# A two-layer sequence trunk on one core: the copy of U on ScalarE alone, betas and keys scaled in place in two buffers

## The chip, the cores and the metric

The kernel runs on one core of one Trainium2 chip. The core has a matrix engine (PE in the profile, with its weight loads as PEld), a vector engine (DVE), a scalar engine (ACT), a general engine (POOL) and a queue that issues most transfers (SP). Each engine works through a list of its own in order and waits on semaphores where it needs another engine's result. The metric is the device time of one execution in microseconds (us). The kernel before took 1878.74 us (median of three runs, 1875.97 to 1879.16).

## The reference

The kernel computes two layers on 1024 positions of 1024 channels, in float32. Layer 0 has two recurrent mixers side by side; layer 1, which the change touches, is a delta rule with 16 heads of 64 channels. After the projections that make r, k, v, the decay w, the rate and the gate, the reference runs one step per position and head:

```python
def step(state, inp):
    r_t, w_t, k_t, v_t, al_t, be_t = inp
    sa = jnp.einsum("bhvk,bhk->bhv", state, al_t)
    state = (state * w_t[:, :, None, :] + sa[..., None] * be_t[:, :, None, :]
             + v_t[..., None] * k_t[:, :, None, :])
    return state, jnp.einsum("bhvk,bhk->bhv", state, r_t)
```

Here `al` is minus the normalised key, called alpha below, and `be` is that key times the rate, called beta. The outputs y then get a group norm, a bonus and a gate, the output projection, a row norm and the residual.

## The kernel before, in words

Layer 1 handles 16 chunks of 64 positions. Inside a chunk the recurrence is solved with matrices. `prep` (line 1144) writes, for each chunk, alphas and receptances to a DRAM tensor `ard` and betas and keys to `bkd`. `invert` (line 1264) inverts a triangular matrix of a chunk by row steps on DVE (lines 1294, 1297, 1303 and 1306), and `merge` (line 1313) finishes it on PE. The inversions are generators that are advanced between the steps of the chunks (`background`, line 1118), and all of them are done before chunk 8.

`chain_phase` (line 1023) runs the chunks one after another. For chunk ch it calls three functions:

- `values(ch + 1)` (line 1386) loads the values and the inverse of the next chunk.
- `gram(ch + 1)` (line 1399) loads `GM` (alphas and receptances) and `BK` (betas and keys) of the next chunk, multiplies them on PE (line 1415, 32 products in two groups of 16), and masks the products on DVE (lines 1420 and 1421). Then POOL multiplies all of `BK` with the decay at the chunk's end, `egc`, and writes the result to another tile, `BS` (line 1425). PE transposes `BS` in eight pieces (line 1430), and ACT copies them to `NK` (line 1431). `BK` and `BS` have one slot each in the pool `cb`, 4 KB per partition.
- `chain(ch)` (line 1434) carries the state. The tile `SV` holds the state of a head on its half of the partitions and values on the other half. PE multiplies it with the masked products (line 1443), ACT copies the result (line 1445), and PE multiplies it with the inverse (line 1458). The result is U, in one bank of PSUM. It replaces the state in `SV`: line 1460 copies the half of the even heads (partitions 0 to 63) with DVE and that of the odd heads with ACT. PE then forms the next state from U, the values and `NK` (line 1465), DVE adds the decayed old state `se` (line 1467), which POOL made (line 1454), and PE completes the outputs (line 1470), which ACT copies (line 1473).

Between these steps run pieces of other work: the gates (line 1013) up to chunk 8, then the group norms (`norm`, line 1479; its small steps are in `rstd2`, lines 201 to 206) and the output projection (`project`, line 1523).

Nobody writes the order of an engine's list by hand. The program opens with `tile.TileContext(nc, schedule_with_timeline_sim=True)` (line 1605): a planner simulates the kernel with durations of its own while it builds it. It puts every instruction into its engine's list when, in that simulation, its inputs and its slot are there, the earlier in the program the sooner. Line 1087 raises the priority of the last two chunks. On the chip each list then runs in that fixed order. A tile of a pool waits for its slot: with one slot, the next chunk's `BK` can be loaded only when the last reader of this chunk's `BK` is done.

Of the kernel before, what the change touches and what calls it, by code (L numbers as in the profile page):

```python
# [7 lines left out]
F32 = mybir.dt.float32  # L8
# [17 lines left out]
# columns of the packed per-channel vectors, eight columns each  # L26
# [6 lines left out]
class Steps:  # L33
    """a generator with the parts that it makes"""
# [11 lines left out]
class Net:  # L46
# [39 lines left out]
    # ---------------------------------------------------------------- constants  # L86
# [15 lines left out]
    def mask_from(self, pool, tmp, name, shape, conds):  # L102
        """uint8 mask, 1 where every affine condition (pattern, base, cm) >= 0 holds."""
        nc = self.nc
        n = 1
        for s in shape:
            n *= s
        m = tmp.tile([P, n], F32, name="mask_f")
        nc.gpsimd.memset(m, 1.0)
        view = m  # L110
        if len(shape) == 2:
            view = m.rearrange("p (a b) -> p a b", b=shape[1])
        for pat, base, cm in conds:
            nc.gpsimd.affine_select(out=view, in_=view, pattern=pat, compare_op=ALU.is_ge, fill=0.0,
                                    base=base, channel_multiplier=cm)
        u = pool.tile([P, n], U8, name=name)
        nc.vector.tensor_copy(u, m)
        return u

    # ---------------------------------------------------------------- weights  # L120
    def weights(self, units):
        """the pool of weights, for these units in this order; a unit is two pieces"""
        self.wp = self.ctx.enter_context(self.pool("wp", 4))
        self.order, self.queue = list(units), []
# [14 lines left out]
    def unit(self):  # L139
        """the next unit of weights in the order of use, its successor on the way"""  # L140
# [11 lines left out]
    def dense_t2(self, w, e, uh, ul, th):  # L152
        """[128 channels, 512 positions] of unit w's e-th column tile, in two steps."""
# [21 lines left out]
    def dense_n(self, w, uh, ul, tt):  # L175
        """[128 positions, 256 channels] of unit w."""
# [12 lines left out]
    def rstd(self, pool, ss, n, scale, eps):  # L189
        """(ss * scale + eps) ** -0.5 on [128, n]."""  # L190
# [6 lines left out]
    def rstd2(self, pool, ss, n, scale, eps):  # L197
        """the same by the square root of the scalar engine and a Newton step"""
# [10 lines left out]
    def norm_rows(self, pool, x, sq):  # L209
        """root-mean-square scale [128,1] of a row tile [128, 1024]."""  # L210
# [5 lines left out]
    # ---------------------------------------------------------------- layer 0  # L216
    def layer0(self):
        tc, nc, a = self.tc, self.nc, self.a
        with ExitStack() as cx:
            uh, ul = ([[self.mx.tile([P, HALF], F32R, name=f"x{n}{th}") for _ in range(KT)] for th in range(2)] for n in "hl")  # L220
            rgk = cx.enter_context(self.pool("rgk", 1))
            with ExitStack() as c2:
# [38 lines left out]
                # the first projections of the next part lie in PSUM until its pools are there  # L261
# [17 lines left out]
    def warm(self, pool, n):  # L279
        """products of zeros that keep the tensor engine's clock up until there is work"""  # L280
# [9 lines left out]
    def hgrn_consts(self, c, hp):  # L290
        nc = self.nc
        # lower bound and its complement, per channel
# [16 lines left out]
        # masks of a 64-block's rows and columns, the same in both halves of the partitions  # L309
# [6 lines left out]
        # (block, group of blocks, source block of a group)  # L316
# [9 lines left out]
    def hgrn_dense(self, c, big, uh, ul, trees):  # L326
        """the projections, in pieces; a tree starts when its queries and keys are there"""
# [61 lines left out]
    def advance(self, gens):  # L389
        """a stage of the first tree, at times one of the second too"""  # L390
# [5 lines left out]
    def hgrn_half(self, hp, stp, th, j, tr, st, diag, lev):  # L396
        """two heads, four blocks of 128 positions each; the heads run in step"""
        nc = self.nc
        # scores, transposed
# [3 lines left out]
        def scores(i, rhs, w, n, b):  # L403
            """products of the sources of a block of 64 with its groups of n blocks of b targets, w blocks apart"""
# [9 lines left out]
        def put(i, ps, w, b, g, s, mask, dst, src):  # L414
            """the blocks dst of every group of g from the slots src of every w, where the mask allows it"""
# [9 lines left out]
        def wider(i, b, pool):  # L425
            """sources with their way through the other half of a block of 2 * b, totals of such blocks"""
# [8 lines left out]
        # positions themselves and next ones  # L435
# [17 lines left out]
        # blocks of 4 * b from such of b: the slots of a group are queries of its blocks 0 to 3 (even ones) and those of  # L453
        # blocks 2, 3, 3 with their ways through block 1, blocks 1 and 2, block 2 (odd ones)
# [57 lines left out]
        for Q, F, K, V, G, row in tr:  # L512
            # keys with positions on partitions
# [54 lines left out]
    def gate_consts(self, c, tmp):  # L568
        """parts of the gates' matrices, a block of 64 channels at a time, both gates of it beside each other: high
        ones against the two parts of the block on the two halves of the partitions, low ones on the block's own half"""  # L570
# [15 lines left out]
    def rglru(self, cx, uh, ul):  # L586
        tc, nc, a = self.tc, self.nc, self.a
        # -8 softplus(-lam) per channel: max(-lam, 0) + log1p(exp(-|lam|))
# [19 lines left out]
        # sigmoids by tanh: sigmoid(z) = (1 + tanh(z / 2)) / 2  # L608
# [11 lines left out]
        for j in range(4):  # L620
# [45 lines left out]
            # the halves of the two sigmoids that are factors, squared  # L666
# [10 lines left out]
    def out0(self, cx):  # L677
# [9 lines left out]
        for th in range(2):  # L687
# [18 lines left out]
            for dh in range(2):  # L706
                ps = [self.pss.tile([P, HALF], F32, name="sm") if dh else self.psd.tile([P, HALF], F32, name="mm") for _ in range(4)]
                for gi, kg in enumerate(order):
                    w = self.unit()
                    # the last unit row tile by row tile, so that the first ones are there early  # L710
# [46 lines left out]
    def finish(self, rp, th, Y, ss):  # L757
        """norms and residual of four row tiles, and their channels on partitions"""
# [29 lines left out]
    def receptance(self, w, j, th, e2):  # L788
        """a column tile of r, in two steps"""
# [6 lines left out]
    # ---------------------------------------------------------------- layer 1  # L796
    def mix(self, p, k, th, out):
        """u + (shifted u - u) * mu for one channel tile and half."""
# [6 lines left out]
    def mix_parts(self, mp, p, th, eng=None):  # L805
        """the same, a channel tile at a step"""
# [13 lines left out]
    def mixes(self, mp, p, th, eng=None):  # L820
        """the parts of one half of a mix, in the slots of that half"""
# [8 lines left out]
    def lora_consts(self):  # L830
        """the first factors of decay and rate, times 1 - mu and times mu"""
# [16 lines left out]
    def lora(self, th):  # L848
        """low-rank decay and rate of one half"""
# [18 lines left out]
    def lora_parts(self, th, x):  # L868
        """the low parts of the decays on the second half of the partitions, those of the rates on the first"""
# [7 lines left out]
    def layer1_consts(self):  # L877
# [6 lines left out]
        # halves for sigmoids by tanh: 1 + (sigmoid - 1) k_a = tanh * k_a / 2 + 1 - k_a / 2  # L884
# [7 lines left out]
    def layer1_proj(self):  # L892
# [12 lines left out]
        with ExitStack() as cx:  # L905
            mp = self.mx
            with ExitStack() as c2:
                lp = c2.enter_context(self.pool("lora", 1))
                # parts of the low-rank factors: high ones twice, against the two parts of the other factor
# [32 lines left out]
                with ExitStack() as c3:  # L942
                    kp = c3.enter_context(self.pool("kp", 2))
                    # selectors that put a head's sum over its channels into its row: norms and bonuses, in them halves, in them heads
# [13 lines left out]
                    # three stages, one slot apart  # L958
# [29 lines left out]
    def pieces(self, piece, hi, lo):  # L988
        """the pieces of a projection, the first halves of two units before their second halves"""
# [10 lines left out]
    def vpiece(self, w, hi, lo, j, tt):  # L1000
        """values of a row tile, and their products with the bonus"""
# [11 lines left out]
    def gpiece(self, w, hi, lo, j, tt):  # L1013
        """gates of a row tile"""
# [8 lines left out]
    def chain_phase(self, cx, mp, vg, n):  # L1023
        """values with the first inversions; then the chunks one after another, among them the gates, the other
        inversions and, from the middle on, the output"""
# [107 lines left out]
    def output_weight(self, dh, i):  # L1133
        """(k, half of the columns) parts of the last weight, in the slots of the mixes"""
# [9 lines left out]
    def prep(self, kp, e, th, pk):  # L1144
# [13 lines left out]
        # sigmoid(z) = (1 + tanh(z / 2)) / 2  # L1158
# [5 lines left out]
        # running decay exponent inside each chunk, twice  # L1164
# [19 lines left out]
        # squared norms of the heads' keys  # L1184
# [11 lines left out]
        # beta . alpha inside the chunks, rows are source positions  # L1196
# [22 lines left out]
    def head_sums(self, kp, e, th, i, x):  # L1219
        """sums over the channels of the two heads, added to the rows of norms (i = 0) or bonuses"""  # L1220
# [9 lines left out]
    def norms(self, kp):  # L1230
        """bonuses with positions on partitions; inverse squared norms, halved, with 32-blocks on partitions"""
# [16 lines left out]
    def invert_consts(self):  # L1248
# [4 lines left out]
        # halved inverse squared norms, 32 positions to a row, in the order of the blocks  # L1253
# [3 lines left out]
        # identity rows of the 16-blocks, eight rows to a partition group  # L1257
# [6 lines left out]
    def invert(self, cp):  # L1264
        """(I - A)^-1, transposed, of two chunks: 32-blocks row by row on the vector engine, the last level on the
        tensor engine."""
# [5 lines left out]
        # columns times their inverse norms, and so those of the inverse  # L1272
# [14 lines left out]
        def solve(yo, nk, ao):  # L1287
            """columns 1..15 of nk blocks of YP from yo on, by the block of BL at ao"""
# [24 lines left out]
    def merge(self, ch):  # L1313
        """the last level of an inversion, on the tensor engine"""
# [38 lines left out]
    # ---------------------------------------------------------------- chunks  # L1353
    def chain_consts(self):
        nc, big = self.nc, self.big
        # causal masks: rows are source positions (twice), columns strict for alpha and inclusive for r
# [29 lines left out]
    def values(self, ch):  # L1386
        """state (or, later, U) on the head's half of the partitions, values on the other"""
# [11 lines left out]
    def gram(self, ch):  # L1399
# [5 lines left out]
        BK = self.big.tile([P, KT, P], F32, name="BK")  # L1405
# [17 lines left out]
        BS = self.big.tile([P, KT, P], F32, name="BS")  # L1423
        eg_ = self.egc[:, ch, :].rearrange("p (e o) -> p e o", o=1).broadcast_to([P, KT, P])
        nc.gpsimd.tensor_mul(BS, BK, eg_)
        NK = self.cc[ch % 2].tile([P, KT, P], F32, name="NK")
        for eg in range(2):
            ps = self.bank("pt").rearrange("p (q t) -> p q t", t=P)
            for q in range(4):
                nc.tensor.transpose(ps[:, q, :], BS[:, eg * 4 + q, :], self.ident)  # L1430
# [3 lines left out]
    def chain(self, ch):  # L1434
# [24 lines left out]
        for h in range(2):  # L1459
            (nc.scalar.copy if h else nc.vector.tensor_copy)(SV[H[h], h], ps[H[h]])  # L1460
# [18 lines left out]
    def norm(self, ch):  # L1479
        """group norm, bonus and gate of a chunk"""  # L1480
# [30 lines left out]
    def turn(self, ch):  # L1511
        """the two parts of a chunk's rows with channels on partitions"""
# [10 lines left out]
    def project(self, tt):  # L1523
        """output projection, norm and residual of a row tile; the next tile is made ready between"""
# [37 lines left out]
def pack(inputs):  # L1562
# [5 lines left out]
    # the value and gate channels in the order (head parity, head pair, channel), and so the rows of the output weight  # L1568
# [41 lines left out]
```

## Time and profile before

| what | value |
|---|---|
| runs | 1878.74 us median, 1875.97 to 1879.16 |
| span of the profiled execution | 1879.1 us, from the first to the last instruction |
| time of the profiled execution | not listed apart; the slowest run shown is 1879.16 us |
| mean granted PE clock | 0.940 |
| DVE, all copies of line 1460 | 16 of 0.675 us, 1398.2 to 1843.2 us |
| ACT, all copies of line 1460 | 16 of 0.580 us, 1399.0 to 1843.9 us |
| POOL, the scalings of line 1425 | 16 of 1.93 us, 1246.7 to 1815.9 us |
| loads of `BK` | 16 of 512 KB, 4.2 us to landing |

The time axis of the profile starts at the first instruction. Layer 0 and the projections take the first 1244 us; the values' projection with the first inversions goes on to about 1362 us, and the chunks run from there to the end. A row of the timeline gives the start, the duration, the engine, the line, the operation, and in brackets the idle time of the engine before it and what ended it. A row of the waits gives the waiting engine and line, what it waited for, the total in us, the number of waits and the longest one.

### The profile page before, as it was taken

The numbers are of one execution on the slowest core, as the hardware profiler recorded it, in microseconds if no ns is written. First come the engines' busy times: TensorE is split into PE (matmuls) and PEld (weight loads), VectorE is DVE, ScalarE is ACT, GpSimd is POOL, SyncE is SP. The second block draws the span as 40 slices with busy tenths as digits, with TensorE's granted clock in tenths as the row PEclk, the third lists the DMA queues.
The fourth block names the chain that finished last, engine by engine and source line by source line (L and its number), as shares of the span: only waits on it lengthen the run. The fifth ranks groups of instructions, "written<-read, shape, count | busy, mean of one in ns | idle before, by whom it ended". The sixth has DMA issues, their size and how long they took to land. (4 is left out here: it accounts for less than half of the span.)

```text
span 1879.1 us, 34525 instructions
## 1 busy us (share of the span) xinstructions
PE 1726.0 (92%) x13394; PEld 1447.4 (77%) x13394; DVE 1353.5 (72%) x2621; ACT 767.7 (41%) x1468; POOL 717.3 (38%) x638
## 2 busy tenths in 40 slices
PE   7989989999899999999999999979788879978888
PEld 6879789787897777777878766669787868867666
DVE  6585483675847889745355686885999999489984
ACT  5322222323226755545454765666452223242221
POOL 5534232333222212465434243555532333373530
PEclk9989999999899999999999999969889889788989
DMA  5101101111022111375332266756344444664531
GB/s 182 46 24 46 56 18 63 46 35 39 19 72 86 50 63 67 124 236 173 101 123 96 90 152 155 176 138 188 101 144 130 141 129 136 181 197 146 163 102 62
DMA packets 177491, 201.79 MB, mean 107 GB/s; under 512 B 91440, under 2 KB 122416, under 8 KB 177328
## 3 DMA queue, kind: packets, MB, share of 16 engines
q1 hardware_dynamic: 176176, 195.39, 34.9%
q0 software_dynamic: 1152, 4.19, 0.7%
q8 instruction: 106, 1.74, 0.4%
q14 instruction: 57, 0.47, 0.1%
HBM read 136.28 MB, written 63.24 MB: 106 GB/s over the span
## 5 line engine op out<-in xcount | busy, mean ns | idle before, releaser
L135 POOL TENSOR_TENSOR wl<-w,wh 128x1024 fp32r<-128x1024 f32 x110 | 275.5, 2511 | 288.7 <-ACT wh L133 280.6
L160 PE MATMUL mm<-xh,wh 128*128 128x512 f32 x768 | 306.8, 400 | 1.4 <-ACT KK L1183 1.4
L162 PE MATMUL mm<-xh,wl 128*128 128x512 f32 x768 | 305.4, 398 | 0.0
L161 PE MATMUL mm<-xl,wh 128*128 128x512 f32 x768 | 304.6, 397 | 0.0
L184 PE MATMUL mm<-wh,xh 128*128 128x256 f32 x560 | 170.6, 305 | 6.0 <-ACT xh L149 4.4
L160 PEld LDWEIGHTS mm<-xh,wh 128*128 128x128 f32 x768 | 145.6, 190 | 37.0 <-issue 3.9
L162 PEld LDWEIGHTS mm<-xh,wl 128*128 128x128 f32 x768 | 146.0, 190 | 35.3 <-issue 5.0
L186 PE MATMUL mm<-wh,xl 128*128 128x256 f32 x560 | 167.5, 302 | 5.0 <-DVE xl L150 4.3
L161 PEld LDWEIGHTS mm<-xl,wh 128*128 128x128 f32 x768 | 145.9, 190 | 33.3 <-issue 3.4
L185 PE MATMUL mm<-wl,xh 128*128 128x256 f32 x560 | 166.3, 297 | 0.0
L133 ACT CAST wh<-w 128x1024 fp32r<-128x1024 f32 x112 | 117.3, 1049 | 115.8 <-PE mm L161 57.1
L1294 DVE TENSOR_TENSOR PR<-YP,BL 128x80 f32<-128x80 f32 (+20 forms) x240 | 125.8, 545 | 14.1 <-POOL BL L1276 12.0
L184 PEld LDWEIGHTS mm<-wh,xh 128*128 128x128 f32 x560 | 115.0, 205 | 9.7 <-ACT xh L149 5.0
L186 PEld LDWEIGHTS mm<-wh,xl 128*128 128x128 f32 x560 | 114.5, 206 | 7.2 <-DVE xl L150 5.4
L185 PEld LDWEIGHTS mm<-wl,xh 128*128 128x128 f32 x560 | 114.9, 205 | 0.7
L184 PE MATMUL po<-wh,xh 128*128 128x256 f32 x256 | 80.8, 316 | 1.3 <-DVE vg L1020 1.3
L1415 PE MATMUL pg<-GM,BK 64*128 64x128 f32 x512 | 64.3, 328 | 17.0 <-DVE RB L1421 11.5
L185 PE MATMUL po<-wl,xh 128*128 128x256 f32 x256 | 79.5, 311 | 0.0
L186 PE MATMUL po<-wh,xl 128*128 128x256 f32 x256 | 78.2, 306 | 0.0
L803 DVE SCALAR_TENSOR_TENSOR mix<-ut,vec,mix 128x512 f32<-128x512 f32 x64 | 57.2, 902 | 27.6 <-ACT mix L802 26.8
L420 DVE COPY_PREDICATED ST<-m_l,sm 64x128 f32<-64x128 uint8 x224 | 72.4, 337 | 5.5
L1415 PEld LDWEIGHTS pg<-GM,BK 64*128 64x128 f32 x512 | 52.5, 222 | 23.0 <-issue 19.0
(374 smaller groups left out, 4355.7 us busy)
## 6 DMA issues: line engine op xcount, KB each, us to landing
w<-in_W SPq DMA_DIRECT2D x112, 512.0 KB, 3.7
ard<-AR SPq DMA_DIRECT2D x16, 512.0 KB, 4.1
BK<-bkd SPq DMA_DIRECT2D x16, 512.0 KB, 4.2
vd<-vg SPq DMA_DIRECT2D x32, 256.0 KB, 2.9
GM<-ard SPq DMA_DIRECT2D x32, 256.0 KB, 4.4
x<-in_x SPq DMA_DIRECT2D x8, 512.0 KB, 10.1
mgd<-sgq SPq DMA_DIRECT2D x16, 256.0 KB, 2.3
ut<-mgd SPq DMA_DIRECT2D x16, 256.0 KB, 4.5
```

Source lines behind the costliest of these rows:

```text
L133: nc.scalar.copy(hi, w)
L135: (nc.vector if first else nc.gpsimd).tensor_sub(lo, w, hi.bitcast(F32))
L160: nc.tensor.matmul(ps, lhsT=wh[:, c:c + P], rhs=a, start=(k == 0), stop=False)
L161: nc.tensor.matmul(ps, lhsT=wh[:, c:c + P], rhs=b, start=False, stop=False)
L162: nc.tensor.matmul(ps, lhsT=wl[:, c:c + P], rhs=a, start=False, stop=(k == KT - 1))
L184: nc.tensor.matmul(ps, lhsT=a, rhs=h, start=(k == 0), stop=False)
L185: nc.tensor.matmul(ps, lhsT=a, rhs=l, start=False, stop=False)
L186: nc.tensor.matmul(ps, lhsT=b, rhs=h, start=False, stop=(k == KT - 1))
L420: nc.vector.copy_predicated(d, m, x)
L803: nc.vector.scalar_tensor_tensor(out, sh, self.v(f"mu{p}", k), out, ALU.mult, ALU.add)
L1294: nc.vector.tensor_mul(pr, fv(YP, yo, kd + [[48, 8], [1, n]]), fv(BL, ao + i, k0 + [[0, 8], [32, n]]))
L1415: nc.tensor.matmul(ps[h][:, q, :], lhsT=BK[hs, eg * 4 + q, :], rhs=GM[hs, h, eg * 4 + q, :], start=True, stop=True)
```

## The change

Three lines of arithmetic change, all in the chunk loop. The copy of U goes through ACT for both halves. POOL writes the scaled betas and keys back into `BK`, and PE transposes `BK`; the tile `BS` is gone. `BK` gets two slots instead of one, so `BK` and `BS` together take as much memory as the two slots do. Comments and docstrings are left out too, which changes no instruction.

```diff
-        BK = self.big.tile([P, KT, P], F32, name="BK")
+        BK = self.big.tile([P, KT, P], F32, name="BK", bufs=2)
         nc.sync.dma_start(out=BK, in_=self.bkd[ch])
...
-        BS = self.big.tile([P, KT, P], F32, name="BS")
         eg_ = self.egc[:, ch, :].rearrange("p (e o) -> p e o", o=1).broadcast_to([P, KT, P])
-        nc.gpsimd.tensor_mul(BS, BK, eg_)
+        nc.gpsimd.tensor_mul(BK, BK, eg_)
         NK = self.cc[ch % 2].tile([P, KT, P], F32, name="NK")
         for eg in range(2):
             ps = self.bank("pt").rearrange("p (q t) -> p q t", t=P)
             for q in range(4):
-                nc.tensor.transpose(ps[:, q, :], BS[:, eg * 4 + q, :], self.ident)
+                nc.tensor.transpose(ps[:, q, :], BK[:, eg * 4 + q, :], self.ident)
             nc.scalar.copy(NK[:, eg * 4:eg * 4 + 4, :], ps)
...
         for h in range(2):
-            (nc.scalar.copy if h else nc.vector.tensor_copy)(SV[H[h], h], ps[H[h]])
+            nc.scalar.copy(SV[H[h], h], ps[H[h]])
```

## The prediction

> **What bounds the kernel now.** I began with the busy times and slices, to see which engine is full where the change acts.
>
> ```profile
> span 1879.1 us, 34525 instructions
> PE 1726.0 (92%) x13394; PEld 1447.4 (77%) x13394; DVE 1353.5 (72%) x2621; ACT 767.7 (41%) x1468; POOL 717.3 (38%) x638
> ...
> DVE  6585483675847889745355686885999999489984
> ```
>
> Each slice is 47 us; the chunk loop takes the last eleven. DVE stands at 9 in most of them, though its share of the whole span is only 72%. So I cut the loop into stretches; columns are length, busy time (instructions) of PE, weight loads, DVE, ACT, POOL, then clock and DMA.
>
> ```profile
> 1362.00:1597.00 235.00, 204.82 (x2926) 185.39 (x2925) 228.94 (x525) 72.08 (x152) 84.51 (x66) 0.88 0.48 136
> 1597.00:1644.00 47.00, 43.28 (x546) 38.87 (x546) 22.96 (x42) 11.91 (x25) 15.65 (x14) 0.78 0.66 182
> 1644.00:1832.00 188.00, 157.40 (x1661) 126.33 (x1661) 167.16 (x283) 50.81 (x112) 90.51 (x67) 0.88 0.50 152
> 1832.00:1879.00 47.00, 38.80 (x221) 28.85 (x221) 23.45 (x55) 9.23 (x25) 4.48 (x3) 0.96 0.18 62
> ```
>
> To 1597 us (chunks 0 to 7, with the inversions between) DVE works 228.94 of 235 us, 97%: it sets the pace. Chunks 9 to 14 have 167.16 of 188, 89%, with PE at 84%. Between (chunk 8) and in the tail DVE is half idle. Next the copy of U, by its line:
>
> ```profile
> L1460 DVE COPY SV<-pc x16: 670/675/683, 1398.2 to 1843.2; 64x512 f32<-64x512 f32 x16
> L1460 ACT COPY SV<-pc x16: 580/580/584, 1399.0 to 1843.9; 64x512 f32<-64x512 f32 x16
> ...
>   DVE SV L1460: 62.8, 13
>   issue: 5.6, 1
>   DVE rv L201: 3.4, 1
>   PE pc L1458: 2.2, 3
> ```
>
> Half of U goes through DVE (0.675 us), half through ACT (0.580 us), and ACT's half begins only after DVE's. ACT stood ready at this copy for 62.8 us in 13 of 16 chunks, waiting for a DVE copy that itself stood in DVE's queue (it waited for its product only 3 times, 2.2 us). Last, who waits behind it on PE, over the loop and then from 1644 us on:
>
> ```profile
> PE pc L1465 <- DVE SV L1460: 20.0, 6, 4.7
> PE pg L1415 <- DVE RB L1421: 11.5, 7, 4.0
> PE pg L1415 <- DMA BK<-bkd: 5.4, 1, 5.4
> ```
> ```profile
> PE pc L1465 <- DVE SV L1460: 11.7, 3, 4.4
> ```
>
> **The change, part by part.**
>
> *U by ScalarE alone.* DVE loses 16 × 0.675 = 10.8 us. What that is worth depends on the stretch. Chunks 0 to 6 copy before 1597 us: 7 × 0.675 × 0.97 = 4.6 us. Chunks 9 to 14: 6 × 0.675 × 0.89 = 3.6 us. Chunks 7, 8 and 15 fall where DVE has gaps; nothing is counted. Together **−8.2 us**. ACT gains 16 × 0.580 = 9.3 us of work. I cost that at nothing: in the two DVE-bound stretches ACT works 72.08 of 235 and 50.81 of 188 us, and the queue now reaches the copy early. Without that cover it would be 9.3 us. The pair of halves shortens from 0.675 + 0.580 to 2 × 0.580 us. Queued behind the pair on ACT are the copies of NK, of the outputs and the gates' sigmoids; ACT leaves the pair earlier than now, so no new wait arises. The 20.0 us that PE loses before L1465 should go, but where DVE is the bound PE only waits elsewhere instead: next late are the masks of the grams (the L1421 row above). I count nothing, with bounds 0 and −11.7 (the late row alone).
>
> *Scaling in place.* Today POOL multiplies BK into BS; the next multiplication waits for the transposes that read BS, or for its load:
>
> ```profile
> L1425 POOL TENSOR_TENSOR BS<-BK,egc x16: 1893/1929/2612, 1246.7 to 1815.9; 128x1024 f32<-128x1024 f32 x16
> ...
>   DMA BK<-bkd: 29.4, 3
>   PE pt L1430: 28.3, 4
> ```
>
> In place, the multiplication must wait until all 32 products of its own chunk's gram have read BK, and the transposes follow. POOL's 16 × 1.93 us stay, later. The tightest place is chunk 7 (a gap of 4.07 us against 1.93; chunk 1, whose transposes overlap its gram now, needs them only 13 us later):
>
> ```profile
> 1575.57 1.45 PE L1415 MATMUL pg<-GM,BK 64*128 64x128 f32 x16
> 1581.09 0.66 PE L1430 MATMUL pt<-ident,BS 128*128 128x128 f32 x4
> ...
> 1580.53 2.15 POOL L1454 TENSOR_TENSOR se<-SV,egc 64x512 f32<-64x512 f32 x2 [9.91 <-DVE SV L1467]
> ```
>
> From 1577.02 to 1581.09 the scaling fits before the transposes and before POOL's next work, `se`, which the chain needs a chunk later. So the wait itself costs nothing; without that cover it would be 1.93 us a chunk.
>
> The time at which POOL multiplies does matter, because DVE and POOL hold each other up. The first and the last scaling in the loop, one between them, and what ran on DVE:
>
> ```profile
> 1411.12 2.26 POOL L1425 TENSOR_TENSOR BS<-BK,egc 128x1024 f32<-128x1024 f32 x1 [7.67 <-PE pt L1430]
> 1411.88 2.44 DVE L1303 TENSOR_TENSOR PR<-YP,BL 128x512 f32<-128x512 f32 x1
> 1722.42 1.90 POOL L1425 TENSOR_TENSOR BS<-BK,egc 128x1024 f32<-128x1024 f32 x1
> 1722.51 1.82 DVE L206 SCALAR_TENSOR_TENSOR rr<-rt,rr 128x1 f32<-128x1 f32 x1
> 1815.86 1.89 POOL L1425 TENSOR_TENSOR BS<-BK,egc 128x1024 f32<-128x1024 f32 x1
> 1815.83 0.67 DVE L1420 TENSOR_TENSOR GM<-pg,gm 64x512 f32<-64x512 f32 x1
> 1816.98 0.78 DVE L205 SCALAR_TENSOR_TENSOR rt<-rt,rv 128x1 f32<-128x1 f32 x1
> ```
> ```profile
> L206 DVE SCALAR_TENSOR_TENSOR rr<-rt,rr x24: 149/167/1820, 1648.4 to 1874.2; 128x8 f32<-128x8 f32 x16, 128x1 f32<-128x1 f32 x8
> 1382.60 1.03 DVE L1303 TENSOR_TENSOR PR<-YP,BL 128x512 f32<-128x512 f32 x1
> ```
>
> L206 takes 0.149 us undisturbed and 1.82 us beside the scaling; L1303 1.03 and 2.44. The mask product L1420, which reads PSUM, runs at its usual 0.67. Summing over the DVE instructions beside the fifteen scalings of the loop (chunk 0's lies earlier, at 1246.7) what each took above an undisturbed one of its shape, I get 15.0 us now (45 instructions, 1411.1 to 1817.9), 1.00 a scaling. After the change all sixteen start where DVE evicts the gram. In the 1.93 us behind each gram's last product, two-SBUF-input instructions hold 11.5 of DVE's 30.7 us (first stretch: the L1303 row above at 1382.60). An estimate: 11.5 / 30.7 × 16 × 1.93 = 11.6 us held, 3.4 less than now, times the 0.9 for which DVE is the bound: **−3.1 us**. Bounds: no hold at all, −15.0; every scaling wholly held, 30.9 − 15.0 = +15.9. I stay near the present row because the place moves only by a few us.
>
> The Trainium skill (SBUF — State Buffer, Who interferes with whom) says that a DVE instruction with two SBUF inputs and a GpSimd instruction that reads SBUF exclude each other for a whole instruction, while one with at most one SBUF input does not contend. The rows agree (1.82 against 0.149 us; L1420 unmoved). It also speaks against the change: a copy out of PSUM is just what POOL can run beside. In this trace such cover is rare:
>
> ```profile
> 1600.79 0.68 DVE L1460 COPY SV<-pc 64x512 f32<-64x512 f32 x1
> 1600.67 1.96 POOL L1425 TENSOR_TENSOR BS<-BK,egc 128x1024 f32<-128x1024 f32 x1 [1.97 <-DMA BK<-bkd]
> ```
>
> Three of the 16 copies (1600.8, 1684.8, 1784.1) lie wholly beside POOL work; giving back the two that I counted makes −7.0 of the −8.2.
>
> *Two buffers.* BK's load no longer waits for the previous chunk's multiplication. Its one cost on PE is in chunk 8:
>
> ```profile
> 1594.32 0.54 SPq L1406 DMA_DIRECT2D BK<-bkd  x1
> 1594.95 1.08 SPq L1404 DMA_DIRECT2D GM<-ard  x2
> 1600.66 0.80 PE L1415 MATMUL pg<-GM,BK 64*128 64x128 f32 x4 [5.44 <-DMA BK<-bkd]
> ```
>
> An earlier BK leaves GM next late: issued 0.6 us behind, needed by the same products. **−0.6 us**, bounds 0 and −5.4.
>
> **Sum.** −8.2 − 3.1 − 0.6 = −11.9. The profiled execution's span, 1879.1, lies with the slowest run shown (1879.16), so next to nothing lies around it; 1867.2 for it, 0.4 less for a median run: **1867 us**, −0.6%.
>
> **The rivals.**
> 1. *The chain's latency pays too.* DVE is not full from 1644 us on, and PE's late waits (11.7 us) become time: 1867 − 11.7 = 1855. For it: ACT's 62.8 us of waiting. Against it: the two engines' shares there, 89 and 84%, leave little room.
> 2. *Hidden.* DVE's queue is written out ahead by a planner with its own durations; the 0.675 us holes become waits for PE or a load, as DVE's 6% of gaps are now. Only the 0.6 us remain: 1878.
> 3. *Slower: the scaling meets the wrong DVE work.* In place, POOL starts behind the gram; if DVE is then in the solve (L1294, L1303) or the norms, the whole 1.93 us is lost 16 times: +15.9 − 8.2 = +7.7, 1886. It decides from a mean hold of (15.0 + 8.2) / 16 = 1.45 us a scaling on; now it is 1.00.
> 4. *A worse list elsewhere.* The planner re-sorts all queues from the first gram on. POOL's other work in the two DVE-bound stretches is 84.51 + 90.51 − 15 × 1.93 = 146 us; at the scalings' rate of 15.0 / 29.0 = 0.52 held per POOL us, a list with 0.63 costs 146 × 0.11 = 16: +4, 1883. Nothing in the profile tells its sign.
>
> **How the numbers follow.** About 0.2% (3.8 us) is what a measurement of this kernel can tell from none. Chances: forecast 0.44 (own range 1859 to 1874), rival 1 0.14, rival 2 0.16 (a quarter of it a small gain), rival 3 0.10, rival 4 0.16 (a quarter of it within 0.2%). Faster 0.44 + 0.14 + 0.04 = 0.62; same 0.12 + 0.04 = 0.16; slower 0.10 + 0.12 = 0.22. The range 1854 to 1885 cuts off half of rivals 1 and 3 and a little of 4.
>
> **What would show it.** Right: no DVE row on U's line; ACT's idle time there shrinking from 72 us to that of PE's product; DVE's busy time 11 to 14 us lower; no wait of PE for U; the scaling's waits going from transposes to the gram, and two-input DVE instructions beside it longer by less than 15.0 us. Wrong: DVE's busy time not lower (rival 3 or 4, told apart by which POOL line it lies beside), or lower by 11 us with the span unchanged (rival 2), or PE stalling at L1465 for ACT.

## The result, and the profile after

The changed kernel takes 1866.86 us (median of 5 runs, 1864.74 to 1867.79); the kernel before takes 1878.74 us beside it (1875.72 to 1880.54). The ratio is 0.993, 95% interval 0.9909 to 0.9952: 13.2 us faster, between 9.0 and 17.1. Differences below are (ratio − 1) × 1878.7 us with the interval in brackets, each from runs of both kernels side by side.

The page of the kernel after, busy times and DVE's slices:

```profile
span 1865.6 us, 34533 instructions
PE 1714.8 (92%) x13394; PEld 1436.2 (77%) x13394; DVE 1326.3 (71%) x2605; ACT 776.5 (42%) x1484; POOL 715.7 (38%) x638
...
DVE  6486484685946898835445486795999999658884
```

DVE lost 27.2 us of busy time (1353.5 to 1326.3), much more than the 10.8 us of copies. The other 16.4 us are probably time for which DVE was held beside POOL, where the new lists put other pairs side by side: e3's expectation has the holds beside POOL's other lines at 80 us before and 63 after. PE does the same 13394 products in 11.2 us less; nothing of PE's own work changed, and the last section comes back to it.

The loop cut where the prediction cut it (length; busy time of PE, weight loads, DVE, ACT, POOL; granted clock of PE; DMA share, GB/s):

```profile
1362.00:1597.00 235.00, 199.21 (x2917) 179.40 (x2915) 224.74 (x525) 74.89 (x154) 83.07 (x62) 0.91 0.48 139
1597.00:1644.00 47.00, 40.52 (x632) 36.92 (x634) 25.45 (x48) 18.02 (x38) 25.04 (x21) 0.85 0.70 198
1644.00:1832.00 188.00, 168.55 (x1653) 131.55 (x1648) 147.58 (x267) 52.43 (x115) 85.97 (x65) 0.90 0.46 146
1832.00:1866.00 34.00, 25.24 (x143) 20.33 (x141) 16.27 (x43) 6.79 (x19) 0.00 (x0) 0.92 0.17 62
```

In the first stretch DVE is still 96% busy (before 97%). From 1644 us on it is at 78% where it was at 89%, and PE at 90% where it was at 84%: there PE is now the fuller engine. The granted clock is 0.91 for 0.88 in the first stretch.

The copy of U and the scaling by their lines: shortest, median and longest duration in ns, first and last start, and below each what the engine idled for. Under the scaling stand, last, those who waited for it.

```profile
L1459 ACT COPY SV<-pc x32: 562/580/585, 1396.5 to 1830.2; 64x512 f32<-64x512 f32 x32
...
  PE pc L1457: 12.5, 7
```
```profile
L1424 POOL TENSOR_TENSOR BK<-BK,egc x16: 1887/1896/2530, 1380.7 to 1802.7; 128x1024 f32<-128x1024 f32 x16
...
  PE pg L1415: 11.7, 3
...
  PE pt L1429: 4.7, 2
```

ACT waits 12.5 us for the product instead of 62.8 us for DVE. POOL waits for the gram (11.7 us) instead of for loads and transposes, and PE now waits for POOL: 4.7 us at the transposes. Before, the scaling kept nobody on PE waiting. PE's longest waits over the loop (1390 to 1850 us; total, times, longest):

```profile
PE pc L1442 <- DVE GM L1420: 7.2, 5, 2.1
PE pg L1415 <- DVE RB L1421: 6.6, 7, 2.3
...
PE pt L1429 <- POOL BK L1424: 4.7, 2, 2.7
```

The 20.0 us before the next state's products (now L1464) are gone, as is the 5.4 us wait for `BK` in chunk 8.

### The profile page after: what moved, and what is told of

The parts are those of the page before. It is cut to its first block, busy times and chain, and to the rows that moved or that the text cites. A ratio compares the mean times of both kernels' runs of the same rounds, so it can differ in the third digit from the quotient of the medians.

```text
span 1865.6 us, 34533 instructions
## 1 busy us (share of the span) xinstructions
PE 1714.8 (92%) x13394; PEld 1436.2 (77%) x13394; DVE 1326.3 (71%) x2605; ACT 776.5 (42%) x1484; POOL 715.7 (38%) x638
## 5 line engine op out<-in xcount | busy, mean ns | idle before, releaser
L1294 DVE TENSOR_TENSOR PR<-YP,BL 128x80 f32<-128x80 f32 (+21 forms) x240 | 125.3, 544 | 14.9 <-POOL BL L1276 12.4
L1453 POOL TENSOR_TENSOR se<-SV,egc 64x512 f32<-64x512 f32 x30 | 33.4, 1115 | 88.6 <-DVE SV L1466 87.2
```

The lines of the kernel that those rows point to most:

```text
L1294: nc.vector.tensor_mul(pr, fv(YP, yo, kd + [[48, 8], [1, n]]), fv(BL, ao + i, k0 + [[0, 8], [32, n]]))
```

## The experiments

The theories. A: the gain is DVE's released time at U (the prediction). B: the gain is the second slot, which lets `BK` come early. C: the scaling meets less two-input work on DVE. D: the planner's list for all engines came out better, and the edits themselves matter little. The kernels in one table (e10 and e11 follow below). "Half clock" is the time from 1362 us to the end of the span in which the granted clock of PE is 0.5, summed from the trace's clock records; "margin" is the mean time from the landing of `BK` to the first product of its gram, chunks 2 to 15.

| kernel | U copied by | keys scaled into | slots of `BK` | difference, us | span, us | margin, us | half clock, us |
|---|---|---|---|---|---|---|---|
| before | DVE, ACT | `BS` | 1 | 0 | 1879.1 | 5.5 | 124.6 |
| after | ACT | `BK` | 2 | −13.2 [−17.1, −9.0] | 1865.6 | 11.1 | 97.3 |
| e1 | ACT | `BS` | 1 | −7.9 [−10.9, −4.7] | 1873.7 | 6.7 | 138.0 |
| e2 | DVE, ACT | `BK` | 2 | −21.8 [−25.6, −17.8] | 1859.6 | 13.2 | 103.8 |
| e3 | ACT, heads swapped | `BK` | 2 | −14.1 [−18.4, −10.0] | 1863.0 | 10.8 | 97.1 |
| e4 | ACT | `BK` | 1 | +3.8 [+0.9, +6.4] | 1880.9 | 0.9 | 135.8 |
| e5 | ACT, DVE | `BK` | 2 | −1.1 [−4.3, +2.3] | 1876.1 | 12.4 | 128.9 |
| e6 | DVE | `BK` | 2 | +1.9 [−1.3, +5.1] | 1884.6 | 11.0 | 130.0 |
| e7 | ACT | `NK` | 2 | −17.5 [−21.8, −13.2] | 1859.0 | 26.2 | 92.5 |
| e8 | ACT | `NK` | 1 | −6.2 [−9.2, −3.2] | 1869.3 | 5.9 | 114.4 |
| e9 | ACT, DVE | `BS` | 1 | −3.9 [−7.7, −0.2] | 1870.9 | 6.3 | 126.6 |
| e12 | ACT, heads swapped | `NK` | 2 | −21.4 [−27.1, −15.6] | 1856.8 | 25.8 | 82.4 |

**e1: U alone.** Against the kernel before:

```diff
-            (nc.scalar.copy if h else nc.vector.tensor_copy)(SV[H[h], h], ps[H[h]])
+            nc.scalar.copy(SV[H[h], h], ps[H[h]])
```

> U by ScalarE alone, scaling as before (BS kept, one slot each). Theory (DVE is the bound, the copy's 0.675 us leave it): 8.2 us below the kernel before, 1870.5 us, DVE busy about 11 us lower, no wait of PE for U. Rival, the chain's latency pays too: 15 to 20 us below, 1859 to 1864 us. Rival, a luckier list: the copies are not what paid, the time is within 3 us of the kernel before although DVE has 10.8 us less of copies.

Measured: 0.9958 (0.9942 to 0.9975), −7.9 us, what the prediction had for this term (−8.2). PE's waits behind U, 20.0 us before, are gone here too, yet not 8.2 + 11.7 us came of it; the end of the interval is −10.9. Other waits took their place (the page's waits of PE, e1, same stretch):

```profile
PE pg L1415 <- DVE RB L1421: 8.5, 6, 4.0
...
PE pg L1415 <- DMA BK<-bkd: 6.9, 2, 5.1
```

**e2: the scaling in place with two slots, U split as before.** Against the kernel after:

```diff
-            nc.scalar.copy(SV[H[h], h], ps[H[h]])
+            (nc.scalar.copy if h else nc.vector.tensor_copy)(SV[H[h], h], ps[H[h]])
```

> Scaling in place with two slots, U still split between DVE and ScalarE. Theory: 3.1 us for fewer holds of DVE beside POOL and 0.6 us for the load, 1875.0 us; the waits of ScalarE and PE for the DVE half of U stay (62 and 20 us). Rival, the scaling meets the wrong DVE work: above the kernel before, up to 1886 us, with over 15 us of holds beside the scalings. Rival, a luckier list: 1867 to 1870 us, as the whole change gives.

Measured: 0.9884 (0.9864 to 0.9905), −21.8 us. That is more than the whole change brings. This half of the change, forecast at −3.7, cannot be a trifle, and the two halves do not add up: U on ACT on top of it costs 8.6 us. So either the copy on ACT hurts, or e2 has a lucky list. The next four kernels are for that.

**e3: both copies on ACT, the heads the other way round.** The work is the same, the planner's order another.

```diff
-        for h in range(2):
+        for h in (1, 0):
             nc.scalar.copy(SV[H[h], h], ps[H[h]])
```

> The changed kernel with the two ScalarE copies of U in the other order: the same work, other lists from the planner. Theory: 1866.9 us within 3 us, since no engine's work changes. Rival, a luckier list (rival 4 of the prediction): off by more than 4 us, with the holds of DVE beside POOL's other lines (63 us in the changed kernel, 80 before) moving by as much.

Measured: 0.9925 (0.9902 to 0.9947), −14.1 us, 0.9 from the kernel after.

**e5: e2 with the two engines exchanged.**

```diff
-            (nc.scalar.copy if h else nc.vector.tensor_copy)(SV[H[h], h], ps[H[h]])
+            (nc.vector.tensor_copy if h else nc.scalar.copy)(SV[H[h], h], ps[H[h]])
```

> Scaling in place with two slots; U split again, but ScalarE copies the even heads and DVE the odd ones: the work of the run that scaled in place only (1859.6 us), with another list. If that run was fast because of what it does (with two slots the gram and NK are late, not U, so taking U off DVE buys nothing and loads ScalarE): 1859.6 us within 3 us. If it had a lucky list: 1864 us or more.

Measured: 0.9994 (0.9977 to 1.0012), −1.1 us: 20.7 us behind e2, with the same work on every engine. Their rows over the same 488 us, e2 first:

```profile
1362.00:1850.00 488.00, 428.03 (x5262) 364.57 (x5262) 414.46 (x877) 138.62 (x295) 193.11 (x146) 0.90 0.48 143
```
```profile
1362.00:1850.00 488.00, 428.60 (x5253) 366.11 (x5252) 415.37 (x868) 140.61 (x294) 196.88 (x146) 0.87 0.48 142
```

PE and DVE agree in busy time within 0.3%, ACT and POOL within 2%. What differs is PE's granted clock, 0.90 and 0.87. Theory D is alive: one exchange of heads is worth more than the change itself.

**e6: both copies on DVE, in place, two slots.**

```diff
-            nc.scalar.copy(SV[H[h], h], ps[H[h]])
+            nc.vector.tensor_copy(SV[H[h], h], ps[H[h]])
```

> Scaling in place with two slots, both halves of U by DVE: 10.8 us more of DVE work than the split copy, 21.6 us more than the changed kernel. Theory of the prediction (DVE's work is the bound, 0.9 of it becomes time): about 10 us above the split copy, 1869 us, and 19 us above the changed kernel if that were the same list, 1886 us. Revised theory (with two slots the gram's loop sets the pace, not DVE's sum): 1858 to 1866 us.

Measured: 1.001 (0.9993 to 1.0027), +1.9 us. Against the kernel after that is 15.1 us for 32 copies of 0.675 us, 21.6 us of DVE's time: 0.7 us per us, near the 0.76 (8.2 / 10.8) of the prediction. Of the two kernels that split U, e5 (−1.1) lies between these ends and e2 (−21.8) outside them. So theory A's size holds with two slots as well, from end to end; for single steps the differences between lists are larger than the term.

**e9: the kernel before with the two engines exchanged.**

```diff
-            (nc.scalar.copy if h else nc.vector.tensor_copy)(SV[H[h], h], ps[H[h]])
+            (nc.vector.tensor_copy if h else nc.scalar.copy)(SV[H[h], h], ps[H[h]])
```

> The kernel before with ScalarE copying the even heads of U and DVE the odd ones: the same work, another list. If lists of the same work differ by some 10 us, as 1859.6 against 1876.7 us suggest: anywhere from 1870 to 1888 us. If the kernel before had an unlucky list (its holds beside POOL add up to 121 us from 1244 us on, those of the changed kernels to 95 to 103): 1868 to 1873 us. If the lists matter little: 1878.7 us within 3 us.

Measured: 0.9979 (0.9959 to 0.9999), −3.9 us. Beside this kernel, e1 gains only 4.0 ± 4.9 us, which may be nothing. So with one slot U's share comes out as 4 or 8 us, by which of two kernels of equal work it is counted from.

**e4: the change with one slot.**

```diff
-        BK = self.big.tile([P, KT, P], F32, name="BK", bufs=2)
+        BK = self.big.tile([P, KT, P], F32, name="BK")
```

> The changed kernel with one slot for BK: its load must now wait for the transposes of the chunk before. Theory: 0.6 us above the changed kernel plus what the later load costs; the load of 4.9 us and the gram behind it then start behind the transposes, which lie 4 to 20 us behind the scaling: 1868 to 1874 us with PE or POOL waiting for BK. Rival, the second slot is worth nothing: 1866.9 us. Rival, the second slot is the whole gain: 1879 us.

Measured: 1.002 (1.0005 to 1.0034), +3.8 us. Taking the second slot away costs 17 us (0.009 ± 0.0026, the half-widths combined as the root of their squares) and the whole gain. Its waits of PE over the loop:

```profile
PE pg L1415 <- DMA BK<-bkd: 17.9, 8, 3.9
PE pg L1415 <- DVE RB L1421: 16.0, 6, 9.0
```

The gram waits for its keys eight times. SP's queue waits before their load for the transposes, eight times too:

```profile
SPq L1406 <- PE pt L1429: 10.3, 8, 2.2
```

One round of the loop that forms, as the timeline has it (start, duration; SPq is SP's queue):

```profile
1494.49 0.33 SPq L1406 DMA_DIRECT2D BK<-bkd  x1
...
1500.04 0.49 PE L1415 MATMUL pg<-GM,BK 64*128 64x128 f32 x4
...
1512.86 1.90 POOL L1424 TENSOR_TENSOR BK<-BK,egc 128x1024 f32<-128x1024 f32 x1 [2.04 <-issue]
...
1522.12 0.60 PE L1429 MATMUL pt<-ident,BK 128*128 128x128 f32 x4
...
1522.79 0.32 SPq L1406 DMA_DIRECT2D BK<-bkd  x1
...
1528.68 1.16 PE L1415 MATMUL pg<-GM,BK 64*128 64x128 f32 x16
```

Load, gram, scaling, transposes, and at once the next load: 28.3 us from load to load, a chunk's period. In place, the transposes too read `BK`, so they end the slot's use.

**e7: the scaled keys written to `NK`, two slots of `BK`.** `NK`'s own tile takes the scaled keys, and their transposes overwrite it later. The scaling need not wait for the gram. Against the kernel after:

```diff
-        nc.gpsimd.tensor_mul(BK, BK, eg_)
         NK = self.cc[ch % 2].tile([P, KT, P], F32, name="NK")
+        nc.gpsimd.tensor_mul(NK, BK, eg_)
...
-                nc.tensor.transpose(ps[:, q, :], BK[:, eg * 4 + q, :], self.ident)
+                nc.tensor.transpose(ps[:, q, :], NK[:, eg * 4 + q, :], self.ident)
```

> The changed kernel, but the scaled keys go to NK's own tile (two of them in turn), not back into BK, so the scaling need not wait for the gram; BK has two slots. If the scaling's wait behind the gram costs nothing, as predicted: 1866.9 us within 3 us. If it is on the path (PE waits 4.7 us for the scaling in the changed kernel): 1860 to 1863 us.

Measured: 0.9907 (0.9884 to 0.993), −17.5 us. PE never waits for the scaling.

**e8: e7 with one slot.**

```diff
-        BK = self.big.tile([P, KT, P], F32, name="BK", bufs=2)
+        BK = self.big.tile([P, KT, P], F32, name="BK")
```

> The same with one slot for BK, so the second slot is the only difference. Revised theory: BK's load must wait for the last product of the gram before, 4 to 5 us of load then lie between two grams: 8 to 15 us above the kernel with two slots, near 1872 us, which U alone on ScalarE took. The prediction's term (0.6 us): the same time as with two slots.

Measured: 0.9967 (0.9951 to 0.9983), −6.2 us. In the program nothing but the slot differs from e7, so the second slot is worth 11.3 ± 5.3 us where the scaling is out of the way, as far as this pair tells. The lists differ too, and e2 and e5 show that lists alone can lie 20.7 us apart. With U on ACT, all four kernels with two slots (−13.2 to −21.4) lie below all three with one (−7.9 to +3.8), which speaks for the slot; with U split, the slots do not separate the kernels (0 and −3.9 with one, −1.1 and −21.8 with two). SP's waits before the load show what one slot waits for, in e8, and in the kernel before:

```profile
SPq L1406 <- PE pg L1415: 7.3, 3, 5.7
```
```profile
SPq L1406 <- PE pg L1415: 4.7, 3, 2.8
```

Where SP waits, it is for the gram's last product. In the kernel before, chunk 7's load follows it at once, at 1553.64, when chunk 6's products end at 1553.57:

```profile
1551.53 2.04 PE L1415 MATMUL pg<-GM,BK 64*128 64x128 f32 x14 [0.56 <-DVE RB L1421]
...
1553.64 0.33 SPq L1406 DMA_DIRECT2D BK<-bkd  x1
```

In the kernel after, chunk 5's load goes out before chunk 4's gram has even begun:

```profile
1474.78 0.33 SPq L1406 DMA_DIRECT2D BK<-bkd  x1
1476.96 1.16 PE L1415 MATMUL pg<-GM,BK 64*128 64x128 f32 x16 [1.29 <-DMA BK<-bkd]
```

Over chunks 2 to 15 the load comes on average 4.4 us after the previous gram's end before, and 4.2 us ahead of it after. The steps e1, e8, e7, after lead from the one kernel to the other: −7.9 (U), +1.7 (`NK` for `BS`), −11.3 (second slot), +4.3 (in place), together −13.2. These steps carry errors of 3 to 6 us each, without the differences between lists. Two slots beside `BS` would be the direct test of the slot; they do not fit in memory and were not tried.

**e10: the scaling on ACT.** It does the same multiplication in eight pieces a chunk, so that no scaling runs beside DVE on POOL. Against the kernel after:

```diff
-        nc.gpsimd.tensor_mul(BK, BK, eg_)
+        for e in range(KT):
+            nc.scalar.mul(BK[:, e, :], BK[:, e, :], self.egc[:, ch, e:e + 1])
```

> The changed kernel with the scaling done by ScalarE, eight products of 128 by 128 with the decay as its scale, instead of POOL. POOL loses 16 x 1.9 us, and the 13.6 us for which DVE is held beside the scalings can go; ScalarE gains about 16 x 8 x 0.3 = 38 us. If DVE's held time is the kernel's time (0.9 of it): 12 us below the changed kernel, 1855 us. If it hides like the rest: 1867 us within 4 us. If ScalarE becomes late (U, NK and the gates queue behind the eight products): above 1872 us.

Measured: 0.9929 (0.9903 to 0.9955), −13.3 us: the same as after. The busy times, and the pieces by their line:

```profile
PE 1720.6 (92%) x13394; PEld 1437.9 (77%) x13394; DVE 1306.9 (70%) x2605; ACT 819.7 (44%) x1612; POOL 686.1 (37%) x622
```
```profile
L1424 ACT ACTIVATE BK<-BK,egc x128: 384/388/406, 1366.6 to 1803.2; 128x128 f32<-128x128 f32 x128
```

DVE's busy time falls by another 19.4 us, among it all 13.6 us of holds beside the scalings, and the time stays. What ACT pays for it (43.2 us more work, mostly under cover) may eat a gain; that was not separated.

**e11: the scaling twice.** The keys are scaled a second time, so the output is not the reference's; it doubles POOL's work there and the holds.

```diff
         nc.gpsimd.tensor_mul(BK, BK, eg_)
+        nc.gpsimd.tensor_mul(BK, BK, eg_)
```

> The changed kernel with each scaling done twice in a row by POOL (the second one is extra, so the state is scaled once too often and the output is another). It adds 16 x 1.9 = 30 us to POOL and, at the present 13.6 us held per 16 scalings, about 14 us of holds to DVE; the transposes start 1.9 us later. If DVE's held time is the kernel's time: 12 us above the changed kernel, 1879 us. If POOL's place behind the gram is covered and the holds hide: 1867 us within 4 us.

Measured: 0.9974 (0.9959 to 0.9989), −4.9 us, so 8.3 ± 4.9 us slower than after. Holds beside the scalings went from 13.6 to 26.1 us, and the transposes come later too. With e10 this leaves theory C without its gain: more holds may cost something, fewer brought nothing here.

**e12: e7 with the heads the other way round.**

```diff
-        for h in range(2):
+        for h in (1, 0):
             nc.scalar.copy(SV[H[h], h], ps[H[h]])
```

> The scaled keys in NK's own tile, two slots for BK, and ScalarE's two copies of U in the other order: the work of the run that took 1859.4 us, another list. If not waiting for the gram is what made that run 7.5 us faster than the changed kernel: 1859 us within 3 us again. If it was its list: near 1867 us, where both lists of the changed kernel lie, or above.

Measured: 0.9886 (0.9856 to 0.9917), −21.4 us, 1857.48 us: with e2 the fastest here, and faster than the kernel after by 8.3 ± 7.0 us. Its page, the scaling by its line, for which nobody on PE waits any more, and PE's longest wait in the loop:

```profile
span 1856.8 us, 34528 instructions
PE 1699.8 (92%) x13394; PEld 1423.6 (77%) x13394; DVE 1315.5 (71%) x2605; ACT 777.2 (42%) x1484; POOL 722.9 (39%) x638
```
```profile
L1425 POOL TENSOR_TENSOR NK<-BK,egc x16: 1890/1904/2626, 1276.4 to 1766.3; 128x1024 f32<-128x1024 f32 x16
```
```profile
PE pg L1415 <- DVE RB L1421: 27.7, 10, 7.5
```

What PE waits for now is the mask on DVE, as the prediction had named it "next late". Against e7 the same work differs by 3.9 us.

## Why the prediction was right, and where it was not

The time, 1867, was right, and that is in good part luck. Two of its terms were wrong, and their errors nearly cancel: the second slot brought −11.3 us where −0.6 was forecast, and the scaling in place +6.0 (the steps +1.7 and +4.3, neither clear of its error) where −3.1 was.

- **"U by ScalarE alone", −8.2: right with one slot, as far as the lists let one see.** e1 measured −7.9. e6 against after gives nearly the rate that came of counting the 0.675 us only where DVE is full. Counted from e9 instead of the kernel before, e1's gain is 4.0 ± 4.9 us. PE's wait behind U was rightly counted as nothing: it went, and waits for the masks and for `BK` came.
- **"Two buffers", −0.6: the mis-sized term.** e8 to e7 measures −11.3 ± 5.3, and e4 to after −17, in place. The step that failed is "BK's load no longer waits for the previous chunk's multiplication". It looked at the multiplication, which was early, and at the one wait of PE for `BK` in the trace. But the slot is also held by the gram's products on PE. In the trace of before they end later than the multiplication in 13 of the chunks 1 to 14, and all 14 loads of chunks 2 to 15 were issued after the previous gram's end. So the term left out the reader that ends last. That the wait shows on PE only once is probably no measure of it, because the queues are written around loads that come late; this is argued, and no single wait shows where in those queues the 11 us lay. The claim that an earlier `BK` leaves `GM` next late failed too: in chunk 8 the load is issued 24 us ahead and the gram starts without any wait.

```profile
1568.23 1.07 SPq L1406 DMA_DIRECT2D BK<-bkd  x1
...
1592.38 1.16 PE L1415 MATMUL pg<-GM,BK 64*128 64x128 f32 x16
```

- **"So the wait itself costs nothing": probably wrong, by 4 to 7 us.** In place against `NK` costs 4.3 ± 6.0 (e7 to after), 7.3 ± 7.1 (e12 to e3), and 10.0 ± 4.1 with one slot (e8 to e4): one sign three times, the first within its error. Chunk 7 was read as the tightest place, in the trace of before. Once the lists were written anew, PE waited for the scaling at two transposes of other chunks (4.7 us), and the transposes held the slot on, as e4 shows: the margin is 11.1 us in place and 26.2 in `NK`. That the wait itself is the price is not shown: in e2 PE waits 15.6 us for the scaling (3 times, the longest 10.4), and e2 is 8.6 us faster than the kernel after.
- **Fewer holds, −3.1: no gain found.** The holds went from 15.0 to 13.6 us, 1.4 of the 3.4 us forecast. e10 takes away the rest of them and gains nothing, and e11 doubles them and loses 8.3 ± 4.9 us. So no run shows the 0.9 of itself at which a hold was priced; e10's extra work on ACT and e11's later transposes leave its true price open.
- **Rival 1** (the latency pays, 1855) falls: e1 has PE's waits gone and −7.9. **Rival 2** (hidden) falls by e6 against after (15.1 ± 5.1 us for the copies); e1 alone excludes it only when counted from the kernel before, not from e9. **Rival 3** falls by its own condition: 13.6 / 16 = 0.85 us a scaling, not 1.45. **Rival 4** (a list) did not happen with its sign, but its size is real: kernels with the same work lie 0.9 (after, e3), 3.9 (before, e9), 3.9 (e7, e12) and 20.7 us (e2, e5) apart. What makes e2 so good is open. The gain of the whole change is larger than what these lists blur: from before or e9 to after or e3 it is between 9 and 14 us.
- **The readings that were to show it.** No DVE row on U's line, ACT's idle time 12.5 us, no wait of PE for U, the scaling's wait on the gram: all came. "DVE's busy time 11 to 14 us lower" came as 27.2, and DVE's busy time does not order the kernels: e4 has 1322.6 and is slow, e2 has 1334.8 and is fast.

## What to carry to other kernels

A buffer's slot is free only after its last reader, so price a second slot by listing every reader and asking which ends last, not by the waits that the trace shows. Where a planner writes the queues, test an edit with its sister of equal work (heads exchanged) before a few microseconds are put down to it. Writing in place saves a buffer but joins two waits, that of the writer for the old readers and that of the slot for the new ones; a tile that is dead at that moment (`NK` here) saves it without either.

## What was not expected of the hardware

PE's granted clock falls after short pauses in the loop, and not for the pause alone. The kernel before, around the 5.44 us for which chunk 8's gram waits; the column after POOL's is the clock:

```profile
1585.00:1595.20 10.20, 10.20 (x177) 9.50 (x176) 9.62 (x25) 3.96 (x9) 6.72 (x8) 1.00 0.66 194
1600.60:1612.00 11.40, 11.34 (x132) 10.00 (x133) 6.14 (x12) 2.41 (x6) 4.58 (x4) 0.50 0.80 251
1612.00:1618.90 6.90, 6.90 (x65) 6.16 (x66) 1.11 (x2) 1.11 (x3) 0.00 (x0) 0.50 0.24 66
1620.00:1630.00 10.00, 10.00 (x147) 9.13 (x147) 1.55 (x3) 3.22 (x6) 0.00 (x0) 1.00 0.37 87
```
```profile
1594.83 0.28 PE L184 MATMUL po<-wh,xh 128*128 128x256 f32 x1
...
1609.76 0.42 PE L185 MATMUL po<-wl,xh 128*128 128x256 f32 x1
```

The clock is 0.5 for 20.5 us (1598.7 to 1619.2), which begin in the pause and go on although PE is busy for 18.24 of 18.30 us from 1600.6 on; a product of the same shape takes 0.42 us for 0.28. By the trace's clock records these stretches come in multiples of 3.4 us, and pauses of 4.6 and 4.7 us (from 1511.3 and 1543.0) go with 10.2 us of them each. The prediction priced that wait at its 5.4 us at most; with 18.5 us of work at half clock behind it, it is up to 9 us of PE's work more. The Trainium skill (TensorE: Matmul & The Clock Gate, Part 1: The HAM clock gate) says that an idle window of about 3.4 us halves the clock, and that about 3.4 us of sustained work restores it. The trace of before agrees only in part. Of its 16 falls from 1373 us on, 4 follow 3.4 us without work, this one among them; before the other 12, PE was busy for 5 to 59% of the last 3.4 us. And of the 15 half-clock stretches that end there, 8 end with their first 3.4 us of (nearly) unbroken work, while 7 go on through one to four more such windows; this one is the longest.

From 1362 us on, half clock fell from 124.6 to 97.3 us; half of the difference, 13.7 us, is about what PE's busy time lost (11.2 us), a likely answer to the question from the beginning. In the kernels of the table and e10 (108.9 us) and e11 (130.8 us) the half-clock time goes with the span (correlation 0.90; 82.4 us in the shortest), and e2 and e5 differ in it by 25.1 us. It is not all: e1 has 13.4 us more of it than the kernel before and is faster. No run separates cause from sign here: a better list has fewer pauses, and both follow from them. That the second slot's 11 us are in good part clock, by taking pauses away, is an argument and not shown.
